# Plain fp32 matmuls in the Fourier transforms of a Hyena branch, in place of three matmuls of split operands

## The chip, the cores and the metric

The kernel runs on one core of one Trainium2 chip. A core has TensorE (PE, matrix products; PEld is its weight load), VectorE (DVE), ScalarE (ACT), GpSimd (POOL) and SyncE (SP, which here issues nearly all DMA transfers). The metric is the device time of one execution in microseconds, as the median of three runs.

## The reference

One layer of an encoder trunk on x of shape (1, 1024, 1024), in fp32. Three token mixers (A: windowed attention, B: Hyena, C: differential attention) read one normed input projection; their outputs are gated, summed and projected, and a SwiGLU feed-forward part follows. The change touches branch B alone:

```python
def hyena_filters(L, w1, b1, f1, w2, b2, f2, w3):
    ...
    h = jnp.sin(f1.astype(f32) * (z @ w1.astype(f32) + b1.astype(f32)))
    h = jnp.sin(f2.astype(f32) * (h @ w2.astype(f32) + b2.astype(f32)))
    h = (h @ w3.astype(f32)).reshape(L, HY_ORDER, HY_DIRS, HY_WIDTH)
    ...
    h = h * decay[:, None, None, :]
    fwd, bwd = h[:, :, 0], h[:, :, 1]
    c = jnp.concatenate([fwd[:1] + bwd[:1], fwd[1:], jnp.zeros_like(fwd[:1]), bwd[1:][::-1]], axis=0)
    return c * lax.rsqrt(jnp.sum(c * c, axis=0, keepdims=True) + RMS_EPS)

def fft_conv(u, cf):
    L = u.shape[1]
    U = jnp.fft.rfft(u.astype(jnp.float32), n=2 * L, axis=1)
    y = jnp.fft.irfft(U * cf[None], n=2 * L, axis=1)[:, :L]
    return y.astype(u.dtype)

def hyena_branch(u, conv_w, conv_b, w1, b1, f1, w2, b2, f2, w3, hy_d):
    L = u.shape[1]
    u = short_conv(u, conv_w, conv_b)
    v, x1, x2 = jnp.split(u, 3, axis=-1)
    cf = jnp.fft.rfft(hyena_filters(L, w1, b1, f1, w2, b2, f2, w3), axis=0)
    z = x1 * (fft_conv(v, cf[:, 0]) + hy_d[0] * v)
    z = x2 * (fft_conv(z, cf[:, 1]) + hy_d[1] * z)
    return z
```

L is 1024, the branch is 512 channels wide, and there are two orders, so two filters and two convolutions of 512 channels.

## The kernel before

**Arithmetic.** Nearly every product is made with fp32r operands, each fp32 operand split into a high and a low part: `split` (lines 98 to 100) lets ScalarE write the rounded high part and VectorE (or GpSimd) subtract it from the source; `mm3` (102 to 105) then makes three matmuls, high by high, high by low, low by high. A matmul of plain F32 tiles is possible too and is used in small places (lines 224, 229, 250, 690).

**The transforms.** A transform of length 2048 is taken apart into a radix-16 stage on VectorE and ScalarE (`fwd`, lines 107 to 159) and dense products with tables of cosines and sines on TensorE (`dft`, 161 to 181). The 512 channels are worked on as two halves of 256. For each half, `fwd` makes four groups of sources: od (two groups, lines 136 and 137), ev (147 to 149) and e0 (151 to 157). `dft` splits a group into rh and rl, loads for each of its two residues a table `ft`, and makes eight products of 128x128 weights by 128x256 into a PSUM tile X, each of them by `mm3`. `filters` (240 to 318) does this for two orders by two halves: it makes the filter in time from the features (line 271 and 272) times a decay table `dec` that is loaded, transforms it, and stores the spectrum H to DRAM (`hd`).

**The convolutions.** `hyena` (495) runs order by order and half by half. `conv` (320 to 398) transforms its input with `fwd`; for each group it loads H, multiplies it with X on VectorE into m1 (328 to 338), splits m1 into yh and yl (340), loads the inverse tables `it` (344) and makes eight products into a PSUM tile V (347 and 348), which VectorE and ScalarE then put together (350 to 398). In all there are 32 forward groups (16 of filters, 16 of convolutions) and 16 inverse ones.

**Tables.** The tables of the forward and inverse transforms come in as inputs `fw` and `iv`, with the high and low parts side by side (384 KB and 512 KB for each of eight residues). At the beginning GpSimd's queue copies `fw` to an F32R tensor in DRAM (1044 to 1046), and in the second filter it copies `iv` (303 to 305); the loads of `ft` and `it` read these copies. SP's queue issues them in order with all other loads and stores.

**What sets the order.** The framework orders instructions per engine when the kernel is built, by priority and by the order of the program; each engine then works its list off in order, waiting on semaphores. Other work of TensorE is put between the transforms by generators: `E.tick(us)` (989 to 995) draws from `E.fill` half-tiles of the Hyena projection (`hyena_proj`, 459 to 485), of the attention projections (`qkv`, 529 to 601) and of the gates (518), until their nominal costs use up the credit. E.rate sets how much is drawn at each tick: 7.0 in the filters, 5.5 in the convolutions. `hyena_proj` makes u with three VectorE operations (463 and after), and for the tiles of v it turns u by eight transposes (`to_slots`, 487). `qkv` collects in `pend` the rope of a half (541) and runs it at the next half's first step.

**Buffers.** Tiles take turns in a number of buffers by tag. In the filters (1057): rh 2, rl 1, ft 2, k4 4, h4 1. In the convolutions (1062): rh 2, rl 1 (yh and yl use them too), ft 2, it 1, k4 4, u8 2. The transforms' PSUM tiles share three buffers (x).

Of the kernel before, what the change touches and what calls it, by code (L numbers as in the profile page):

```python
# [17 lines left out]

def f22(x):
    x=np.asarray(x,np.float32); u=x.view(np.uint32).astype(np.uint64)  # L20
    u=(u+0x7FF+((u>>12)&1))&~np.uint64(0xFFF)
    return u.astype(np.uint32).view(np.float32)
def hilo(m):
    h=f22(m.astype(np.float32)); l=f22((m-h.astype(np.float64)).astype(np.float32))
    return h,l

def dft_tables():
    n1=np.arange(128)[:,None]; k1=np.arange(128)[None,:]
    fw=np.zeros((8,128,6,128),np.float32)
    iv=np.zeros((8,128,4,256),np.float32)  # L30
    for r in range(1,8):
        ph=2*PI*(n1*(16*k1+r)%2048)/2048
        c,s=np.cos(ph),np.sin(ph)
        ch,cl=hilo(c); sh,sl=hilo(s)
        for i,m in enumerate((ch,cl,sh,sl,-sh,-sl)): fw[r,:,i,:]=m
        g=2.0/2048
        yr=np.concatenate([g*c.T,-g*s.T],1); yi=np.concatenate([g*s.T,g*c.T],1)
        for i,m in enumerate(hilo(yr)+hilo(yi)): iv[r,:,i,:]=m
    kk=np.arange(64)[None,:]
    p0=2*PI*(n1*(16*kk)%2048)/2048; p8=2*PI*(n1*(16*kk+8)%2048)/2048  # L40
    alt=1.0-2.0*(np.arange(128)%2)
    c0,s0,c8,s8=np.cos(p0),np.sin(p0),np.cos(p8),np.sin(p8)
    s0n=s0.copy(); s0n[:,0]=alt

    for i,m in enumerate(hilo(np.concatenate([c0,c8],1))+hilo(np.concatenate([s0n,s8],1))): fw[0,:,i,:]=m
    g=2.0/2048
    z=np.zeros((64,128))
    w=np.full((64,1),g); w[0]=g/2
    yr=np.concatenate([np.concatenate([w*c0.T,z],0),np.concatenate([z,g*c8.T],0)],1)
    yi=np.concatenate([np.concatenate([w*s0n.T,z],0),np.concatenate([z,g*s8.T],0)],1)  # L50
    for i,m in enumerate(hilo(yr)+hilo(yi)): iv[0,:,i,:]=m
    return fw,iv

def dft_tables2():
    fw,iv=dft_tables()
    f=np.zeros((8,128,768),np.float32)
    f[1:]=fw[1:].reshape(7,128,768)
    p=np.zeros((128,4,192),np.float32)
    p[:,:,0:64]=fw[0,:,0:4,0:64]; p[:,:,128:192]=fw[0,:,0:4,64:128]
    f[0]=p.reshape(128,768)  # L60
    return f,iv.reshape(8,128,1024)
def filt_tables():
# [18 lines left out]
def dma(nc,dst,src):  # L81
    f=lambda t: t.bitcast(F32) if t.dtype==F32R else t
    nc.sync.dma_start(f(dst),f(src))
# [77 lines left out]
def dft(nc,E,pool,gi,src):  # L161

    hi=pool.tile([128,2,2,256],F32R,tag="rh",name="rh"); lo=pool.tile([128,2,2,256],F32R,tag="rl",name="rl")
    split(nc,hi,lo,src,E.loeng(gi))
    X=E.px.tile([128,2,2,256],F32,tag="x",name="X")
    for i,r in enumerate(GROUPS[gi]):
        t=pool.tile([128,768],F32R,tag="ft",name="ft")
        dma(nc,t,E.fw[r])
        if r==0:
            w=t.rearrange("p (a b) -> p a b",b=192)  # L170
            for k,(a,b) in enumerate(((0,1),(2,3))):
                mm3(nc,X[:,i,k,:],w[:,a,0:128],w[:,b,0:128],hi[:,0,0,:],lo[:,0,0,:],True,False)
                mm3(nc,X[:,i,k,:],w[:,a,64:192],w[:,b,64:192],hi[:,1,0,:],lo[:,1,0,:],False,True)
        else:
            w=t.rearrange("p (a b) -> p a b",b=128)
            R=(hi[:,0,i,:],lo[:,0,i,:]); J=(hi[:,1,i,:],lo[:,1,i,:])
            mm3(nc,X[:,i,0,:],w[:,0],w[:,1],R[0],R[1],True,False)
            mm3(nc,X[:,i,0,:],w[:,4],w[:,5],J[0],J[1],False,True)
            mm3(nc,X[:,i,1,:],w[:,0],w[:,1],J[0],J[1],True,False)
            mm3(nc,X[:,i,1,:],w[:,2],w[:,3],R[0],R[1],False,True)  # L180
    return X
# [58 lines left out]
def filters(tc,nc,E,a,h2):  # L240
    V=nc.vector
    if True:
      with tc.tile_pool(name="fl",bufs=1,reuse_waits="tile",side="right") as fl_:
# [8 lines left out]
        for o in range(2):  # L252
          for u in range(2):
# [42 lines left out]
            def consume(gi,X):  # L296
                H=fl.tile([128,2,2,256],F32,tag="h4",name="H")
                nc.scalar.copy(H,X)
                if gi==3:
                    dma(nc,E.hd[o][u][1:128,4096:4352],H[1:128,0,0,:])  # L300
                    dma(nc,E.hd[o][u][0:1,4096:4352],H[0:1,0,1,:])
                    z=nc.gpsimd.memset(H[0:1,0,1,:],0.0)
                    if o==0 and u==1:
                        with tc.issue_after(z.ins):
                            for r in range(8): nc.gpsimd.dma_start(E.iv[r],a['iv'][r])
                dma(nc,E.hd[o][u][:,1024*gi:1024*gi+1024],H.rearrange("p a b c -> p (a b c)"))
# [13 lines left out]
def conv(nc,E,cv,u8,o,u,ysb):  # L320
# [3 lines left out]
    def consume(gi,X):  # L324
# [13 lines left out]
        V.tensor_tensor(m1[:,:,1,:],m1[:,:,1,:],m2[:,:,0,:],op=ALU.add)  # L338
        yh=cv.tile([128,2,2,256],F32R,tag="rh",name="yh"); yl=cv.tile([128,2,2,256],F32R,tag="rl",name="yl")
        split(nc,yh,yl,m1,E.loeng(gi))  # L340
        P=E.px.tile([128,2,2,256],F32,tag="x",name="V")
        for i,r in enumerate(GROUPS[gi]):
            t=cv.tile([128,4,256],F32R,tag="it",name="it")
            dma(nc,t.rearrange("p a b -> p (a b)"),E.iv[r])
            for c in range(2):
                s=slice(128*c,128*c+128)
                mm3(nc,P[:,i,c,:],yh[:,i,0,s],yl[:,i,0,s],t[:,0],t[:,1],True,False)
                mm3(nc,P[:,i,c,:],yh[:,i,1,s],yl[:,i,1,s],t[:,2],t[:,3],False,True)
        E.tick(E.rate)
# [109 lines left out]
def hyena_proj(tc,nc,E,prep,a,hT):  # L459
# [3 lines left out]
    STT=lambda o,a,s,b: V.scalar_tensor_tensor(o,a,s,b,op0=ALU.mult,op1=ALU.add)  # L463
    st={}
    for t,h in [(4,0),(5,0),(4,1),(5,1)]+[(t,h) for t in (6,7,8,9,0,1,2,3,10,11) for h in range(2)]:
# [13 lines left out]
        if h:  # L479
            if t<4:  # L480
                dma(nc,E.vc[0][t//2][:,t%2,:],u)
                to_slots(nc,E,E.gp,E.px.tile([128,8,128],F32,tag="x",name="pv"),u,lambda s: dma(nc,E.vd[t//2][:,:,128*(t%2):128*(t%2)+128],s))
            else:
                dma(nc,E.x12[(t-4)//2][:,t%2,:],u)
        yield 5.45

# [42 lines left out]
def qkv(tc,nc,E,prep,a,hT,pool):  # L529
# [37 lines left out]
    def group(c0,nh,T,qk,vd):  # L567
# [3 lines left out]
        for h in range(2):  # L571
            X=E.gp.tile([128,4,4,64],F32,tag="gt",name="X")
            if vd: vh=pool.tile([128,4,128*n],F32R,tag="th",name="vh"); vl=pool.tile([128,4,128*n],F32R,tag="tl",name="vl")
            for tp in range(2):
                p=E.pg.tile([128,2,256],F32,tag="g",name="pN")
                for t in range(2):
                    for q in range(4):
                        s=slice(256*tp+128*t,256*tp+128*t+128)
                        for k in range(2):
                            mm3(nc,p[:,t],hT[h][0][:,2*q+k,s],hT[h][1][:,2*q+k,s],W[q][0][:,k],W[q][1][:,k],q+k==0,q+k==4)  # L580
                ts=slice(2*tp,2*tp+2)
                with tc.high_priority(HP):
                    nc.scalar.copy(X[:,ts].rearrange("p t s d -> p t (s d)"),p)
                if vd: split(nc,vh[:,ts],vl[:,ts],X[:,ts,nh:4].rearrange("p t s d -> p t (s d)"),nc.gpsimd)
                if tp==0:
                    while pend: pend.pop()()
                yield 5.76
            if vd:
                for i in range(n):
                    for d,v in zip(vd[i],(vh,vl)): dma(nc,d[:,4*h:4*h+4],v[:,:,128*i:128*i+128])  # L590
            if nh: pend.append(lambda h=h,X=X: rope(h,X[:,:,0:nh],T,qk))
    pend=[]
    for gn,jobs in (('qn_c',[(3+i,4,[E.cqk[2*i+j][0] for j in range(2)],None) for i in range(2)]),
# [5 lines left out]
        for c0,nh,qk,vd in jobs:  # L599
            yield from group(c0,nh,T,qk,vd)  # L600
    pend.pop()()

# [381 lines left out]
def encoder(tc,a,out):  # L984
    nc=tc.nc
    E=E_()
    E.loeng=lambda gi: nc.vector
    E.fill=[]; E.credit=0.0; E.rate=0.0
# [14 lines left out]
    with ExitStack() as top:  # L1003
# [3 lines left out]
        E.hd=[[D(f"hd{o}{u}",[128,4352]) for u in range(2)] for o in range(2)]  # L1007
        E.fw=[D(f"fw{r}",[128,768],F32R) for r in range(8)]; E.iv=[D(f"iv{r}",[128,1024],F32R) for r in range(8)]
        E.vd=[D(f"vd{u}",[128,8,256]) for u in range(2)]
# [23 lines left out]
        with ExitStack() as z:  # L1033
            feat=[]; mlp=filter_mlp(tc,nc,E,a,fst,feat)
            m0=pool(z,"m0",{'xt':8,'xn':2,'ssr':3,'ssq':2})
            late=m0.tile([128,1],F32,tag="late",name="late")
            xs=[]
            with tc.high_priority(3*HP):
                for i in range(8):
                    t=m0.tile([128,1024],F32,tag="xt",name="xt"); dma(nc,t,x[128*i:128*i+128]); xs.append(t)  # L1040
                    if i==0:
                        dma(nc,E.ident,a['ident'])
                        g=m0.tile([128,1024],F32,tag="g",name="g"); dma(nc,g,a['norm1_g'].broadcast_to([128,1024]))
            seen=nc.gpsimd.tensor_copy(late,xs[7][:,0:1])
            with tc.issue_after(seen.ins):
                for r in range(8): nc.gpsimd.dma_start(E.fw[r],a['fw'][r])
            next(mlp)
# [5 lines left out]
        with ExitStack() as hy:  # L1053
            qp=pool(hy,"qp",{'m2':1,'ssq':2,'ssr':3,'th':1,'tl':1})
            D0=hyena_proj(tc,nc,E,prep,a,hT); D2=qkv(tc,nc,E,prep,a,hT,qp); D1=gates(tc,nc,E,prep,a,hT)
            E.fill=[D0,D2,D1]
            E.flb={'k4':4,'u8':2,'wr':1,'wa':2,'wb':2,'k2':4,'k2a':2,'h4':1,'rs':3,'rh':2,'rl':1,'ft':2,'fg':1,'od':1}
            E.rate=7.0
            filters(tc,nc,E,a,feat)
            fst.close()  # L1060
            drain(D0)
            cv=pool(hy,"cv",{'u8':2,'k2':11,'k4':4,'h4':1,'rh':2,'rl':1,'ft':2,'it':1,'fg':1,'od':1},side="right")
            E.rate=5.5
# [73 lines left out]
def tables():  # L1137
    t={}
    t['fw'],t['iv']=dft_tables2()
    t['zT'],t['decay']=filt_tables()  # L1140
# [21 lines left out]
```

## Time and profile before

| what | value |
|---|---|
| median of 3 runs | 2219.35 us (2217.25 to 2220.83) |
| the profiled execution | 2214.34 us |
| its span, first to last instruction | 2212.6 us |
| busy: PE, PEld, DVE, ACT, POOL | 1980.1, 1658.8, 1414.3, 876.0, 444.6 us |
| mean granted TensorE clock | 0.960 |

The times below are those of the profiled execution. In a row of the profile the line number is that of the kernel before; where a helper makes the instruction (L99 and L100 for `split`, L103 to L105 for `mm3`, L83 for the DMAs), the tiles tell which call it is: `X<-rh,ft` is a product of a forward transform, `V<-it,yh` one of an inverse one. A row "A <- B: 27.1, 11, 10.6" says that A stood idle for 27.1 us in 11 times, until B was done, 10.6 us the longest time. In a row of the order in time the columns are start, duration, engine, line, instruction, tiles (out<-in), shape, and in brackets the idle time just before it with what ended it. In the view of busy time by stretch, each engine has its busy time and in brackets its number of instructions; the last columns are the granted clock, the share of the time in which the DMA engines were busy, and the rate.

### The profile page before, as it was taken

What the parts mean: (1) busy time and instruction counts of PE and PEld (TensorE: products, weight loads), DVE (VectorE), ACT (ScalarE), POOL (GpSimd) and SP (SyncE); (2) the same over time, 40 slices, a digit from 0 to 9 for tenths busy, and PEclk for the clock granted to TensorE, in tenths of its full rate; (3) what the DMA queues carried; (4) which work ended last, traced back from release to release, by engine and by line L of the source; (5) the groups of instructions that cost most, each with busy time, mean ns of one, the idle gap of its engine ahead of it and who ended that gap; (6) DMA issues with size and microseconds to landing.
All of it is one profiled execution on the core that took longest, in us unless ns stands there. A gap on an engine that the chain in (4) does not pass through costs nothing. (4 is left out here: it accounts for less than half of the span.)

```text
span 2212.6 us, 27550 instructions
## 1 busy us (share of the span) xinstructions
PE 1980.1 (89%) x10597; PEld 1658.8 (75%) x10597; DVE 1414.3 (64%) x2019; ACT 876.0 (40%) x1371; POOL 444.6 (20%) x302
## 2 busy tenths in 40 slices
PE   6986888888868999899879988899699999999999
PEld 4775788888867778677668766699488888888887
DVE  7875777775775654642467877534856656557674
ACT  5433333333332222765666654234422222223332
POOL 2532232212141112432000023400210110101000
PEclk9999999999989999999889999899799999999999
DMA  5457536575556556334354342444222322248333
GB/s 194 143 189 244 191 94 221 163 228 183 179 202 204 188 177 189 95 103 92 94 157 118 119 135 72 147 166 159 67 95 96 110 105 100 95 157 313 116 109 104
DMA packets 141454, 327.28 MB, mean 148 GB/s; under 512 B 18518, under 2 KB 44616, under 8 KB 139530
## 3 DMA queue, kind: packets, MB, share of 16 engines
q1 hardware_dynamic: 140810, 318.17, 44.6%
q0 software_dynamic: 512, 7.34, 0.9%
q8 instruction: 83, 1.36, 0.3%
q14 instruction: 49, 0.40, 0.1%
HBM read 237.65 MB, written 95.16 MB: 150 GB/s over the span
## 5 line engine op out<-in xcount | busy, mean ns | idle before, releaser
L427 POOL TENSOR_TENSOR wlo<-wraw,whi 128x512 fp32r<-128x512 f32 x96 | 142.0, 1482 | 625.4 <-ACT whi L426 590.4
L103 PE MATMUL pT<-hT,whi 128*128 128x512 f32 x576 | 233.8, 406 | 19.1 <-DVE u L463 10.6
L105 PE MATMUL pT<-hT,wlo 128*128 128x512 f32 x576 | 232.3, 403 | 0.0
L104 PE MATMUL pT<-hT,whi 128*128 128x512 f32 x576 | 231.7, 402 | 0.6 <-DVE hT L100 0.6
L426 ACT ACTIVATE whi<-wraw 128x512 fp32r<-128x512 f32 (+1 forms) x148 | 99.5, 675 | 217.5 <-PE pT L104 110.0
L103 PE MATMUL pN<-whi,hT 128*128 128x256 f32 x576 | 164.5, 286 | 12.3 <-ACT whi L426 12.0
L104 PE MATMUL pN<-wlo,hT 128*128 128x256 f32 x576 | 164.5, 286 | 5.6 <-DVE wlo L427 5.5
L105 PE MATMUL pN<-whi,hT 128*128 128x256 f32 x576 | 163.5, 285 | 0.0
L103 PE MATMUL fp<-S,bh 128*128 128x512 f32 x352 | 141.5, 402 | 7.7 <-ACT bh L99 7.7
L103 PEld LDWEIGHTS pT<-hT,whi 128*128 128x128 f32 x576 | 112.1, 195 | 45.1 <-issue 18.1
L105 PE MATMUL fp<-S,bh 128*128 128x512 f32 x352 | 139.0, 395 | 0.0
L104 PE MATMUL fp<-S,bh 128*128 128x512 f32 x352 | 139.0, 395 | 0.0
L104 PEld LDWEIGHTS pT<-hT,whi 128*128 128x128 f32 x576 | 112.0, 194 | 24.8 <-issue 1.5
L105 PEld LDWEIGHTS pT<-hT,wlo 128*128 128x128 f32 x576 | 111.7, 194 | 23.1
L103 PEld LDWEIGHTS pN<-whi,hT 128*128 128x128 f32 x576 | 112.5, 196 | 13.7 <-ACT whi L426 13.2
L105 PE MATMUL fo<-w2h,gA 128*128 128x512 f32 x308 | 119.8, 389 | 0.0
L104 PE MATMUL fo<-w2h,gA 128*128 128x512 f32 x308 | 119.8, 389 | 0.0
L103 PE MATMUL fo<-w2h,gA 128*128 128x512 f32 x308 | 119.7, 389 | 0.0
L104 PEld LDWEIGHTS pN<-wlo,hT 128*128 128x128 f32 x576 | 112.7, 196 | 6.7 <-DVE wlo L427 6.6
L105 PEld LDWEIGHTS pN<-whi,hT 128*128 128x128 f32 x576 | 112.7, 196 | 0.0
L103 PE MATMUL X<-rh,ft 128*128 128x256 f32 x256 | 79.1, 309 | 37.5 <-ACT rh L99 27.1
L99 ACT ACTIVATE bh<-t 128x1024 fp32r<-128x1024 f32 x44 | 46.5, 1059 | 145.3 <-PE fp L104 142.8
(347 smaller groups left out, 5395.4 us busy)
## 6 DMA issues: line engine op xcount, KB each, us to landing
wraw<-in_w SPq DMA_DIRECT2D x108, 256.0 KB, 3.2
ft<-fw SPq DMA_DIRECT2D x64, 384.0 KB, 4.2
graw<-gs SPq DMA_DIRECT2D x35, 512.0 KB, 3.5
it<-iv SPq DMA_DIRECT2D x32, 512.0 KB, 3.7
gd<-gt SPq DMA_DIRECT2D x24, 512.0 KB, 3.0
gt<-gd SPq DMA_DIRECT2D x24, 512.0 KB, 3.2
wraw<-in_ffn_w SPq DMA_DIRECT2D x22, 512.0 KB, 3.7
r<-in_ffn_w SPq DMA_DIRECT2D x22, 512.0 KB, 3.6
```

Of the source, the lines that this page charges most:

```text
L99: nc.scalar.activation(hi,src,AF.Identity)
L103: nc.tensor.matmul(p,lh,rh,start=first,stop=False)
L104: nc.tensor.matmul(p,lh,rl,start=False,stop=False)
L105: nc.tensor.matmul(p,ll,rh,start=False,stop=last)
L426: nc.scalar.activation(hi,raw,AF.Identity)
L427: (eng or nc.vector).tensor_tensor(lo,raw,hi.bitcast(F32),op=ALU.subtract)
```

## The change

The forward products, the inverse products and their tables become plain fp32. The tables hold each value once (192 KB and 256 KB for a residue in place of 384 KB and 512 KB) and are read from the inputs; the two copies on GpSimd's queue, with the small copy that the first one waited for, are gone. `dft` takes the source group itself as the moving operand, and `conv` takes m1 as the stationary one: rh, rl, yh and yl, with 48 splits, no longer exist. Each `mm3` there becomes one matmul call.

Buffers change with it. Filters: k4 6, h4 2, ft 3, no rh and rl. Convolutions: u8 3, k4 5, it 2, no rh and rl.

Two steps are issued later than before: in `hyena_proj` the transposes of a finished tile of v come after the first half-tile of the next tile, and in `qkv` the rope of a half comes at the second step of the next half instead of its first, and one rope at a time, oldest first.

The features and the weights of the filters (lines 232 to 236, 259 to 263) are split as before, as are all other products.

```diff
@@ def dft_tables():
-    fw=np.zeros((8,128,6,128),np.float32)
-    iv=np.zeros((8,128,4,256),np.float32)
+    fw=np.zeros((8,128,384)); iv=np.zeros((8,128,2,256))
...
-        ch,cl=hilo(c); sh,sl=hilo(s)
-        for i,m in enumerate((ch,cl,sh,sl,-sh,-sl)): fw[r,:,i,:]=m
...
+        fw[r]=np.concatenate([c,s,-s],1)
@@ def dft(nc,E,pool,gi,src):
-    hi=pool.tile([128,2,2,256],F32R,tag="rh",name="rh"); lo=pool.tile([128,2,2,256],F32R,tag="rl",name="rl")
-    split(nc,hi,lo,src,E.loeng(gi))
     X=E.px.tile([128,2,2,256],F32,tag="x",name="X")
+    mm=nc.tensor.matmul
     for i,r in enumerate(GROUPS[gi]):
-        t=pool.tile([128,768],F32R,tag="ft",name="ft")
+        t=pool.tile([128,384],F32,tag="ft",name="ft")
         dma(nc,t,E.fw[r])
...
-            R=(hi[:,0,i,:],lo[:,0,i,:]); J=(hi[:,1,i,:],lo[:,1,i,:])
-            mm3(nc,X[:,i,0,:],w[:,0],w[:,1],R[0],R[1],True,False)
-            mm3(nc,X[:,i,0,:],w[:,4],w[:,5],J[0],J[1],False,True)
-            mm3(nc,X[:,i,1,:],w[:,0],w[:,1],J[0],J[1],True,False)
-            mm3(nc,X[:,i,1,:],w[:,2],w[:,3],R[0],R[1],False,True)
+            R,J=src[:,0,i,:],src[:,1,i,:]
+            mm(X[:,i,0,:],t[:,0:128],R,start=True,stop=False)
+            mm(X[:,i,0,:],t[:,256:384],J,start=False,stop=True)
+            mm(X[:,i,1,:],t[:,0:128],J,start=True,stop=False)
+            mm(X[:,i,1,:],t[:,128:256],R,start=False,stop=True)
@@ def filters(tc,nc,E,a,h2):
-                    z=nc.gpsimd.memset(H[0:1,0,1,:],0.0)
-                    if o==0 and u==1:
-                        with tc.issue_after(z.ins):
-                            for r in range(8): nc.gpsimd.dma_start(E.iv[r],a['iv'][r])
+                    nc.gpsimd.memset(H[0:1,0,1,:],0.0)
@@ def conv(nc,E,cv,u8,o,u,ysb):
-        yh=cv.tile([128,2,2,256],F32R,tag="rh",name="yh"); yl=cv.tile([128,2,2,256],F32R,tag="rl",name="yl")
-        split(nc,yh,yl,m1,E.loeng(gi))
...
-            t=cv.tile([128,4,256],F32R,tag="it",name="it")
+            t=cv.tile([128,2,256],F32,tag="it",name="it")
...
-                mm3(nc,P[:,i,c,:],yh[:,i,0,s],yl[:,i,0,s],t[:,0],t[:,1],True,False)
-                mm3(nc,P[:,i,c,:],yh[:,i,1,s],yl[:,i,1,s],t[:,2],t[:,3],False,True)
+                nc.tensor.matmul(P[:,i,c,:],m1[:,i,0,s],t[:,0],start=True,stop=False)
+                nc.tensor.matmul(P[:,i,c,:],m1[:,i,1,s],t[:,1],start=False,stop=True)
@@ def hyena_proj(tc,nc,E,prep,a,hT):
-                to_slots(nc,E,E.gp,E.px.tile([128,8,128],F32,tag="x",name="pv"),u,lambda s: dma(nc,E.vd[t//2][:,:,128*(t%2):128*(t%2)+128],s))
+                pend.append(lambda t=t,u=u: to_slots(nc,E,E.gp,E.px.tile([128,8,128],F32,tag="x",name="pv"),u,lambda s: dma(nc,E.vd[t//2][:,:,128*(t%2):128*(t%2)+128],s)))
...
+        elif pend: pend.pop()()
@@ def qkv(tc,nc,E,prep,a,hT,pool):
-                if tp==0:
-                    while pend: pend.pop()()
+                if tp==1 and pend: pend.pop()()
...
-            if nh: pend.append(lambda h=h,X=X: rope(h,X[:,:,0:nh],T,qk))
+            if nh: pend.insert(0,lambda h=h,X=X: rope(h,X[:,:,0:nh],T,qk))
@@ def encoder(tc,a,out):
-        E.fw=[D(f"fw{r}",[128,768],F32R) for r in range(8)]; E.iv=[D(f"iv{r}",[128,1024],F32R) for r in range(8)]
+        E.fw=[a['fw'][r] for r in range(8)]; E.iv=[a['iv'][r] for r in range(8)]
...
-            seen=nc.gpsimd.tensor_copy(late,xs[7][:,0:1])
-            with tc.issue_after(seen.ins):
-                for r in range(8): nc.gpsimd.dma_start(E.fw[r],a['fw'][r])
...
-            E.flb={'k4':4,'u8':2,'wr':1,'wa':2,'wb':2,'k2':4,'k2a':2,'h4':1,'rs':3,'rh':2,'rl':1,'ft':2,'fg':1,'od':1}
+            E.flb={'k4':6,'u8':2,'wr':1,'wa':2,'wb':2,'k2':4,'k2a':2,'h4':2,'rs':3,'ft':3,'fg':1,'od':1}
...
-            cv=pool(hy,"cv",{'u8':2,'k2':11,'k4':4,'h4':1,'rh':2,'rl':1,'ft':2,'it':1,'fg':1,'od':1},side="right")
+            cv=pool(hy,"cv",{'u8':3,'k2':11,'k4':5,'h4':1,'ft':2,'it':2,'fg':1,'od':1},side="right")
```

More of the change, by code (lines that the diff above doesn't have):

```diff
@@ L17 @@
 SLOT=[0,1,2,3,4,7,6,5]
[L19 to L25, printed above, removed]
 def dft_tables():
     n1=np.arange(128)[:,None]; k1=np.arange(128)[None,:]
-    fw=np.zeros((8,128,6,128),np.float32)
-    iv=np.zeros((8,128,4,256),np.float32)
+    fw=np.zeros((8,128,384)); iv=np.zeros((8,128,2,256))
+    g=2.0/2048
     for r in range(1,8):
@@ L33, in dft_tables @@
         c,s=np.cos(ph),np.sin(ph)
-        ch,cl=hilo(c); sh,sl=hilo(s)
-        for i,m in enumerate((ch,cl,sh,sl,-sh,-sl)): fw[r,:,i,:]=m
-        g=2.0/2048
-        yr=np.concatenate([g*c.T,-g*s.T],1); yi=np.concatenate([g*s.T,g*c.T],1)
-        for i,m in enumerate(hilo(yr)+hilo(yi)): iv[r,:,i,:]=m
+        fw[r]=np.concatenate([c,s,-s],1)
+        iv[r,:,0]=np.concatenate([g*c.T,-g*s.T],1); iv[r,:,1]=np.concatenate([g*s.T,g*c.T],1)
     kk=np.arange(64)[None,:]
     p0=2*PI*(n1*(16*kk)%2048)/2048; p8=2*PI*(n1*(16*kk+8)%2048)/2048
-    alt=1.0-2.0*(np.arange(128)%2)
     c0,s0,c8,s8=np.cos(p0),np.sin(p0),np.cos(p8),np.sin(p8)
[L43 to L61, printed above, removed]
+    s0[:,0]=1.0-2.0*(np.arange(128)%2)
+    o=np.zeros((128,64))
+    fw[0]=np.concatenate([c0,o,c8,s0,o,s8],1)
+    z=np.zeros((64,128)); w=np.full((64,1),g); w[0]=g/2
+    iv[0,:,0]=np.concatenate([np.concatenate([w*c0.T,z],0),np.concatenate([z,g*c8.T],0)],1)
+    iv[0,:,1]=np.concatenate([np.concatenate([w*s0.T,z],0),np.concatenate([z,g*s8.T],0)],1)
+    return fw.astype(np.float32),iv.reshape(8,128,512).astype(np.float32)
 def filt_tables():
@@ L161, in dft @@
 def dft(nc,E,pool,gi,src):
-    hi=pool.tile([128,2,2,256],F32R,tag="rh",name="rh"); lo=pool.tile([128,2,2,256],F32R,tag="rl",name="rl")
-    split(nc,hi,lo,src,E.loeng(gi))
     X=E.px.tile([128,2,2,256],F32,tag="x",name="X")
+    mm=nc.tensor.matmul
     for i,r in enumerate(GROUPS[gi]):
-        t=pool.tile([128,768],F32R,tag="ft",name="ft")
+        t=pool.tile([128,384],F32,tag="ft",name="ft")
         dma(nc,t,E.fw[r])
         if r==0:
[L170 to L173, printed above, removed]
-        else:
-            w=t.rearrange("p (a b) -> p a b",b=128)
-            R=(hi[:,0,i,:],lo[:,0,i,:]); J=(hi[:,1,i,:],lo[:,1,i,:])
-            mm3(nc,X[:,i,0,:],w[:,0],w[:,1],R[0],R[1],True,False)
-            mm3(nc,X[:,i,0,:],w[:,4],w[:,5],J[0],J[1],False,True)
-            mm3(nc,X[:,i,1,:],w[:,0],w[:,1],J[0],J[1],True,False)
-            mm3(nc,X[:,i,1,:],w[:,2],w[:,3],R[0],R[1],False,True)
+            for k in range(2):
+                mm(X[:,i,k,:],t[:,192*k:192*k+128],src[:,0,0,:],start=True,stop=False)
+                mm(X[:,i,k,:],t[:,192*k+64:192*k+192],src[:,1,0,:],start=False,stop=True)
+        else:
+            R,J=src[:,0,i,:],src[:,1,i,:]
[3 more added lines that the diff above has]
+            mm(X[:,i,1,:],t[:,128:256],R,start=False,stop=True)
     return X
@@ L463, in hyena_proj @@
     STT=lambda o,a,s,b: V.scalar_tensor_tensor(o,a,s,b,op0=ALU.mult,op1=ALU.add)
-    st={}
+    st={}; pend=[]
     for t,h in [(4,0),(5,0),(4,1),(5,1)]+[(t,h) for t in (6,7,8,9,0,1,2,3,10,11) for h in range(2)]:
@@ L600, in qkv @@
             yield from group(c0,nh,T,qk,vd)
-    pend.pop()()
+    while pend: pend.pop()()
 def load_stack(nc,dst,src,swap=False):
@@ L986, in encoder @@
     E=E_()
-    E.loeng=lambda gi: nc.vector
     E.fill=[]; E.credit=0.0; E.rate=0.0
@@ L1035, in encoder @@
             m0=pool(z,"m0",{'xt':8,'xn':2,'ssr':3,'ssq':2})
-            late=m0.tile([128,1],F32,tag="late",name="late")
             xs=[]
@@ L1138, in tables @@
     t={}
-    t['fw'],t['iv']=dft_tables2()
+    t['fw'],t['iv']=dft_tables()
     t['zT'],t['decay']=filt_tables()
```

## The prediction

> **What bounds the kernel now.** I read three views: where the transforms lie in time and the busy time of each engine by stretch; then TensorE's own waits between 100 and 860 us; then the order in time at a few places.
>
> ```profile
> L103 PE MATMUL X<-rh,ft x256: 274/283/584, 111.0 to 815.1; 128*128 128x256 f32 x128
> L105 PE MATMUL V<-it,yl x128: 277/282/415, 405.2 to 835.5; 128*128 128x256 f32 x128
> ```
> ```profile
> core 0: us, PE busy (x) PEld busy (x) DVE busy (x) ACT busy (x) POOL busy (x), PEclk, DMA share, GB/s
> 100.00:360.00 260.00, 212.38 (x1316) 188.07 (x1317) 181.47 (x240) 94.92 (x142) 79.33 (x58) 0.93 0.55 181
> 360.00:700.00 340.00, 278.72 (x2065) 262.94 (x2065) 243.82 (x372) 106.11 (x170) 85.65 (x55) 0.93 0.60 196
> 700.00:850.00 150.00, 141.58 (x716) 118.41 (x715) 88.75 (x143) 41.81 (x68) 27.68 (x18) 0.97 0.56 184
> ```
>
> The products into X (forward transforms) and V (inverse ones) lie between 111 and 836 us: filters up to about 360, convolutions after that. In the three stretches TensorE (PE) is busy 632.7 of 750 us and idle 117.3; VectorE (DVE) is busy 514.0. Neither is full: TensorE takes its work in a fixed order and stands still when the next operand is late. What comes after 850 us holds nothing of the change and starts when the convolutions are done, so I move it as a block. What the idle time is made of (us in total, times, the longest):
>
> ```profile
> PE X L103 <- ACT rh L99: 27.1, 11, 10.6
> PE pN L103 <- ACT whi L426: 12.0, 5, 5.2
> PE V L103 <- DMA it<-iv: 11.1, 12, 2.5
> PE pv L489 <- DVE u L463: 10.9, 1, 10.9
> PE pT L103 <- DVE u L463: 10.6, 3, 6.4
> PE pt L561 <- POOL X L556: 10.2, 6, 3.7
> PE X L103 <- DMA ft<-fw: 9.0, 10, 2.4
> ...
> PE X L104 <- DVE rl L100: 5.1, 4, 2.2
> ...
> PE V L105 <- DVE yl L100: 2.3, 3, 1.3
> PE V L103 <- ACT yh L99: 1.9, 3, 1.2
> ```
>
> The splits (rh, rl, yl, yh) hold 36.4 us of it, the table loads (it, ft) 20.1.
>
> **TensorE: two passes for three, but dearer ones.** Records overlap (0.28 us long and 0.12 apart below), so I count from start to start.
>
> ```profile
> 136.84 0.28 PE L271 MATMUL pc<-wa,hs 128*128 128x256 f32 x1
> ...
> 137.79 0.40 PE L105 MATMUL pT<-hT,wlo 128*128 128x512 f32 x1
> 138.02 0.39 PE L103 MATMUL pT<-hT,whi 128*128 128x512 f32 x1
> ...
> 138.72 0.50 PE L250 MATMUL pn<-ones,q 128*128 128x1 f32 x4
> 139.09 0.48 PE L103 MATMUL pT<-hT,whi 128*128 128x512 f32 x1
> ```
> ```profile
> 1130.72 1.02 PE L690 MATMUL prs<-odg,one 128*128 128x512 f32 x2
> 1131.58 0.60 PE L659 MATMUL T<-ident,e 128*128 128x128 f32 x4
> ```
>
> From 136.84 to 137.79 eight fp32r passes of 256 columns start (seven are left out): 0.119 us each. A pass of 512 takes 0.23. The plain fp32 matmul L690 is one call in the code and two records, with 0.86 us for both: 0.43 per pass of 512. The trace has no plain pass of 256 columns. It can't be less than that of one column: the two plain matmuls of L250 are four such passes in 0.37 us, about 0.09 each. It can't be more than the 0.43 of 512. I take half of that, 0.215, since the fp32r pass halves too (0.23 to 0.119). One product then costs 2 x 0.215 = 0.43 where three passes cost 0.357. There are 256 products into X and 128 into V (the counts above), so 384 x 0.073 = 28 us more; at the granted clock of 0.93 about **+30 us**. The ends: 2 x 0.09 makes each product 0.18 cheaper (-68 us), 2 x 0.43 makes it 0.50 dearer (+193). The value taken lies by the nearest row, the 512-column one of the same kind, and I give the ends little chance.
>
> **The splits.** Each transform group loses an activation and a subtraction:
>
> ```profile
> L99 ACT ACTIVATE rh<-od x16: 1041/1052/1062, 109.9 to 761.4; 128x1024 fp32r<-128x1024 f32 x16
> L100 DVE TENSOR_TENSOR rl<-od,rh x16: 1209/1224/2843, 111.1 to 768.6; 128x1024 fp32r<-128x1024 f32 x16
> L99 ACT ACTIVATE rh<-ev x8: 1043/1058/1062, 118.6 to 791.4; 128x1024 fp32r<-128x1024 f32 x8
> L100 DVE TENSOR_TENSOR rl<-ev,rh x8: 1209/1215/1228, 122.0 to 793.5; 128x1024 fp32r<-128x1024 f32 x8
> L99 ACT ACTIVATE rh<-e x8: 1042/1056/1064, 123.0 to 810.2; 128x1024 fp32r<-128x1024 f32 x8
> L100 DVE TENSOR_TENSOR rl<-e,rh x8: 1215/1226/1716, 127.9 to 811.3; 128x1024 fp32r<-128x1024 f32 x8
> ```
> ```profile
> L99 ACT ACTIVATE yh<-m x16: 1040/1060/1067, 402.8 to 820.6; 128x1024 fp32r<-128x1024 f32 x16
> L100 DVE TENSOR_TENSOR yl<-m,yh x16: 1212/1225/1227, 403.9 to 823.9; 128x1024 fp32r<-128x1024 f32 x16
> ```
>
> (Durations: least/median/most, in ns.) VectorE loses 48 subtractions of 1.22 us, 59 us; ScalarE 48 activations of 1.05, 50 us. In what TensorE waits for, the hop goes but not what stands ahead of it. The longest wait shows this:
>
> ```profile
> 653.87 1.74 DVE L137 TENSOR_TENSOR od<-A,B 128x1024 f32<-128x1024 f32 x1
> 656.73 1.74 DVE L100 TENSOR_TENSOR rl<-od,rh 128x1024 fp32r<-128x1024 f32 x1 [1.12 <-ACT rh L99]
> ```
>
> od ends at 655.6 and the product starts only 1.1 us later, after 10.6 us of idle time; od itself was late, and od will be the name of the wait afterwards. The ten other waits of rh mean (27.1 - 10.6)/10 = 1.65 us, not far above the hop's own length. So I take from the 36.4 us: 9.3 for rl, yl and yh less 1; 1.1 of the longest; and 12 of the other 16.5, hence **-21 us** (ends: 0 if od and m are as late as rh and yh were, and -36). VectorE's 59 us come free on an engine that is 69% busy here (514.0 of 750). Of the waits on things that pass through VectorE or ScalarE beside the transforms (whi, and u before pT: 12.0 + 10.6 = 22.6) I take a third: **-8** (ends 0 and -23).
>
> **Tables from the inputs.** Two copies on GpSimd's queue go: fw early, iv beside the second filter. The second shows what it costs:
>
> ```profile
> 200.00:219.00 19.00, 8.06 (x36) 6.47 (x35) 4.84 (x5) 5.28 (x9) 4.54 (x9) 0.80 0.93 320
> ```
> ```profile
> DVE c L275 <- DMA dec<-in_decay: 15.1, 2, 9.3
> ```
> ```profile
> iv<-in_iv POOLq DMA_DIRECT2D x8, 512.0 KB, 8.4
> ```
>
> In these 19 us the DMA engines are 93% busy, the filters' decay tables come late, VectorE stands for 15.1 us in the same window, and TensorE behind it is busy 8.06 us; the 10.9 us wait for u (pv L489) is its end. The copy reads 4.2 MB and writes as much. Without it, and with the transposes pv set one half-tile later by the change, I expect **-13 us**: the 10.9, and some of the half-speed clock (0.80) after it. Ends: -4, if hd, decay and weights crowd the queues anyway, and -15. The early copy I cost at nothing: no row among the waits names it.
>
> **Buffers and moved steps.** `it` gets a second buffer and its load is half as long, `ft` is halved and has three buffers in the filters: of their 20.1 us I take **-16** (ends -8, -20). SP's queue, which issues all loads in order, is also held less by them. The rope of a half is issued one step later and one at a time: of the 10.2 us for `X L556` **-4** (ends +4, since transposes that come later may meet other work, and -10). A buffer now held longer is od, m, ev or e0 (until the products have run, in place of until the split): the convolutions have five k4 buffers for four, the filters six for four, and the pool of one od is refilled only at the next transform, so I cost this at nothing; if that cover is missing, VectorE waits some 0.6 us per group (a group's eight products, 3.4 us for 2.9), 48 x 0.6 = 29 us on an engine with slack.
>
> **The clock and new waits.** The granted clock of 0.93 in 100 to 700 means 14% of the time at half speed. If idle time falls by half, some 0.02 of it comes back on 491 us of busy TensorE: **-8** (ends 0, -20). Against that, where a stall goes the next operand is late: od, m, H, weights (whi). I give back **+8** (ends 0, +25).
>
> Sum: 30 - 21 - 8 - 13 - 16 - 4 - 8 + 8 = **-32 us**. The profiled execution takes 2214.34 us, its span 2212.6; the median shown is 2219.35, 5 us above. I add the sum to the median: **2187 us** (profiled: 2182).
>
> **The rivals.**
> 1. *The waits only change name* (od for rh, m for yh): VectorE's chain sets the pace, as the 10.6 us wait shows in one place. Then +30 stands against the copy (-13), the tables (-16) and a little of the rest (-8): 2212. For it: VectorE is 69% busy in chains. Against it: that chain loses rl and yl, 59 us.
> 2. *TensorE nearly full*: all named waits of splits and tables go, the clock stays up, and weights come early: 30 - 36 - 20 - 13 - 15 - 15 = -69, so 2150. It has for it that 117 us are idle; against it, that many waits have a second cause close behind.
> 3. *Slower, as TensorE is the bound where the stage is packed.* In 700 to 850 it is idle 8.4 of 150 us, and there nothing hides dearer passes. If filters and convolutions run as packed after the change because the scheduler's order puts the same fillers between them, the 30 us count whole and only the tables' waits go partly (-10): 2239. It decides from the point at which less than 30 of the 117 us are won back.
> 4. *Weight loads that no longer hide.* Each plain pass loads its own weights, 768 against 1152 times. If 0.09 us (L250) came on top of every pass: 768 x 0.09 = 69 us on the forecast, 2256. L690 speaks against it: its second load is inside the 0.86 us. The Trainium skill ("TensorE: Matmul & The Clock Gate", section "Weight-path perf modes") says that the fast weight load is off for FP32 inputs, which speaks for slower loads here; by its figure for a load, 128 columns at 1.2 per ns, one would take 0.107 us (an estimate). The trace agrees in size (0.09 in L250), and that still lies under a pass of 0.215.
>
> **How the numbers follow.** Forecast (-32, from -50 to -12): 0.60. Rival 1: 0.17. Rival 2: 0.12. Rival 3: 0.08. Rival 4: 0.03. The range reaches from between rival 2 and the forecast, 2160, to just past rival 1, 2215; outside are most of rival 2 and rivals 3 and 4. A measurement of this kernel can tell some 0.2% (4.4 us) from no change. Of rival 1, 0.06 falls within that; slower are rivals 3 and 4 and a bit of 1, 0.12; faster is the rest, 0.82.
>
> **What would show it.** Records into X and V: 768 in place of 1152, 0.21 us apart (0.12 or 0.43 would be the bounds). No rh, rl, yh, yl; TensorE's waits for od and m should be under 16 us together; over 30 is rival 1. No stretch near 200 us with TensorE under half busy; waits for it and ft under 5 us. VectorE's busy time in the three stretches lower by about 59 us, ScalarE's by 50. The last V some 32 us before 835.5, and what follows shifted as a block; if the part after 850 changes its length by more than 6 us, my frame is wrong.

## The result, and the profile after

The changed kernel takes 2160.8 us (median of 4 runs, 2157.19 to 2163.98), the kernel before 2220.09 beside it: a ratio of 0.9734, 95% interval 0.9713 to 0.9755. The forecast was 2187 us with a range of 2160 to 2215. The time lies 0.8 us inside the fast end of the range, less than the width of the interval, and the gain of 59 us is nearly twice the 32 forecast. Rival 2 of the prediction had 2150 us, nearer to the measured time than the forecast is. The profiled execution has a span of 2158.6 us.

The page's busy times (us, share of the span, instructions):

```profile
PE 1986.1 (92%) x10213; PEld 1657.4 (77%) x10213; DVE 1341.5 (62%) x1971; ACT 839.4 (39%) x1331; POOL 438.7 (20%) x285
```

The same three stretches as before; the last V now starts at 767.9 us:

```profile
100.00:360.00 260.00, 222.98 (x1215) 193.31 (x1214) 168.45 (x234) 81.08 (x129) 84.04 (x54) 0.93 0.44 146
360.00:700.00 340.00, 310.94 (x2023) 285.91 (x2023) 242.65 (x405) 93.34 (x163) 90.01 (x56) 0.96 0.57 187
700.00:850.00 150.00, 145.98 (x658) 119.13 (x657) 60.38 (x131) 47.83 (x89) 35.74 (x23) 1.00 0.51 149
```
```profile
L317 PE MATMUL V<-it,m x128: 378/379/483, 387.6 to 767.9; 128*128 128x256 f32 x128
```

TensorE is idle 70.1 us in them where it was idle 117.3 (the times are the same, the work in them is not: the changed kernel is further along). From 200 to 220 us, where the hole was, it is busy the whole time. Its waits between 100 and 790 us:

```profile
PE pt L531 <- POOL X L526: 19.5, 4, 9.6
PE pT L80 <- DVE u L432: 13.5, 3, 5.6
PE pN L81 <- DVE wlo L396: 6.5, 3, 3.3
PE X L151 <- issue: 6.5, 5, 2.8
PE pN L80 <- ACT ss L225: 5.4, 1, 5.4
PE X L151 <- DVE od L113: 2.8, 2, 2.2
...
PE V L317 <- DVE m L309: 1.6, 1, 1.6
PE X L151 <- DMA ft<-in_fw: 1.1, 1, 1.1
PE V L316 <- DVE m L308: 1.0, 1, 1.0
```

Where rh, rl, yl and yh held 36.4 us, od and m hold about 5, or about 12 if the 6.5 us of X are theirs too, for which the profile names nothing that was waited for ("issue"); the wait for `it` is gone, that for `ft` nearly. What grew most is the wait of the rope's transposes (pt, 10.2 to 19.5). The products into X and V are 768 records where they were 1152. A plain pass, in the order in time of TensorE (start, duration, and two passes to a row):

```profile
388.10 0.59 PE L316 MATMUL V<-it,m 128*128 128x256 f32 x2
388.53 0.59 PE L317 MATMUL V<-it,m 128*128 128x256 f32 x2
388.96 0.59 PE L316 MATMUL V<-it,m 128*128 128x256 f32 x2
```

Each product takes 0.43 us, as half of the 512-column pass had said.

**The end of the transforms moves further than the end of the kernel.** The last V starts 835.5 - 767.9 = 67.6 us earlier, the span ends 54.0 us earlier. The matmuls pT (Hyena's and the gates' projections, the fillers) up to the last V and behind it, before and then after the change:

```profile
0.00:835.50 835.50, 270.66 (x1080) 207.38 (x1081) 36.90 (x60) 31.29 (x57) 0.94 0.57 187
835.50:2212.60 1377.10, 167.89 (x648) 121.84 (x648) 0.00 (x0) 15.79 (x27) 0.97 0.39 124
```
```profile
0.00:767.90 767.90, 237.19 (x960) 185.24 (x961) 37.17 (x60) 28.46 (x52) 0.95 0.49 163
767.90:2158.60 1390.70, 199.85 (x768) 142.71 (x768) 0.00 (x0) 18.92 (x32) 0.97 0.40 125
```

120 of them (120 x 0.23 = 27.6 us) have slid past the last V. They are all that slid: the count of all matmul records behind it grows by 119 (6243 to 6362). The rest of the program is 1390.7 - 1377.1 = 13.6 us longer. So of the 67.6 us, 27.6 is filler that had not been done yet, and the rest of the program takes half of that into its own gaps.

### The profile page after: what moved, and what is told of

Read it like the earlier page. It is cut to its first block, busy times and chain, and to the rows that moved or that the text cites. A ratio compares the mean times of both kernels' runs of the same rounds, so it can differ in the third digit from the quotient of the medians.

```text
span 2158.6 us, 26632 instructions
## 1 busy us (share of the span) xinstructions
PE 1986.1 (92%) x10213; PEld 1657.4 (77%) x10213; DVE 1341.5 (62%) x1971; ACT 839.4 (39%) x1331; POOL 438.7 (20%) x285
## 4 chain that ended last, share of the span: by engine, by line
PE 50%; DVE 5%; ACT 2%; POOL 2%; DMA 2%; issue 1%; SPq 0%; POOLq 0%; ACTq 0%; DVEq 0%
PE fp L82 5%; PE fp L81 5%; PE fp L80 5%; PE fo L82 3%; PE fo L81 3%; PE fo L80 3%; PE S L614 2%; PE f L82 2%; PE f L81 2%; PE f L80 2%; PE pw L81 1%; PE pw L82 1%; PE pw L80 1%; PE pT L81 1%; PE pT L80 1%; PE pT L82 1%
## 5 line engine op out<-in xcount | busy, mean ns | idle before, releaser
L615 DVE TENSOR_REDUCE mx<-S 128x1 f32<-128x1024 f32 x64 | 77.9, 1220 | 46.6 <-PE S L614 45.8
```

What stands on the lines that cost most here:

```text
L615: V.reduce_max(mx[:,c:c+1],S,axis=AX.X)
```

## The experiments

All times are medians, the ratios are against the kernel before on the same chip, with 95% intervals. The changed kernel itself stands at 0.9734.

**The two moved steps.** First both undone, in the changed kernel:

```diff
-                pend.append(lambda t=t,u=u: to_slots(...))
+                to_slots(...)
-        elif pend: pend.pop()()
...
-                if tp==1 and pend: pend.pop()()
+                if tp==0:
+                    while pend: pend.pop()()
...
-            if nh: pend.insert(0,lambda h=h,X=X: rope(h,X[:,:,0:nh],T,qk))
+            if nh: pend.append(lambda h=h,X=X: rope(h,X[:,:,0:nh],T,qk))
```

> The changed kernel (2160.8 us) with its two moved steps put back: the transposes pv right after the tile u, the rope at the next half's first step, all that wait at once. Theory A (the moves are worth little, the gain is in splits, copy and buffers): 2155 to 2168. The wait of pt for POOL X, 19.5 us in the changed kernel and 10.2 before, goes back to about 10, and the wait of pv for u grows from 2.4 us to about 8. Rival (the moved steps made part of the gain that the forecast missed, 27 us): 2172 or more.

Measured: 2196.77 us, 0.9889 (0.986 to 0.9918). The moves were worth some 36 us of the 59, in this kernel: the rival, and more than it asked for. The wait of pt did not go back to 10 us but rose to 45.9; that of pv for u is 7.2, as expected. Then only the rope put back:

```diff
-                if tp==1 and pend: pend.pop()()
+                if tp==0:
+                    while pend: pend.pop()()
...
-            if nh: pend.insert(0,lambda h=h,X=X: rope(h,X[:,:,0:nh],T,qk))
+            if nh: pend.append(lambda h=h,X=X: rope(h,X[:,:,0:nh],T,qk))
```

> The changed kernel with only the rope put back to the next half's first step; the transposes pv stay late. Theory B (the 45.9 us of waits of pt for POOL X with both moves undone are the price): 2185 to 2198, with that wait at 40 us or more. Rival (the transposes pv, which stand in TensorE's order in the filters, are the price): 2158 to 2170.

Measured: 2189.27 us, 0.9868 (0.9849 to 0.9887). So 28 us belong to the rope alone, and the transposes pv have what is left of the 36, about 7, which the intervals don't separate from nothing. The waits of TensorE in this run:

```profile
PE pt L531 <- POOL X L526: 44.7, 10, 7.8
PE pT L80 <- DVE u L432: 12.7, 3, 5.2
```

44.7 us for pt where the kernel before had 10.2 and the changed one 19.5: the difference of 25 us to the changed kernel is nearly the whole price of 28. The same steps moved in the kernel before:

> The kernel before with only the two moved steps of the change (transposes pv one half-tile later, one rope at a time at the second step). Theory B (the moves are worth what their undoing cost, 36 us, on their own): 2180 to 2190. Rival (the moves pay only where the splits are gone, since in the kernel before other waits, rh and it, stand in the same places): 2208 to 2222.

Measured: 2204.64 us, 0.994 (0.9922 to 0.9959), which is 13 us by the ratio (16 by the medians) and between the two theories. The waits there:

```profile
PE X L103 <- ACT rh L99: 19.5, 8, 4.9
...
PE V L103 <- DMA it<-iv: 13.7, 12, 4.0
...
PE pt L562 <- POOL X L557: 3.3, 3, 2.5
```

In the kernel before, the rope's result is waited for 10.2 us; with the rest of the change in and the rope where it was, for 44.7. So the move is worth more in the changed kernel (36 us, both steps) than in the kernel before (13 us). A likely reading is that TensorE in the kernel before stands for the splits and the tables in the same stretches, and that the rope catches up meanwhile. No run tests this alone: that would take the old place of the rope with the splits' hop still there.

**The buffers.** All numbers of before, in the changed kernel:

```diff
-{'k4':6,'u8':2,...,'h4':2,'rs':3,'ft':3,'fg':1,'od':1}
+{'k4':4,'u8':2,...,'h4':1,'rs':3,'ft':2,'fg':1,'od':1}
-{'u8':3,'k2':11,'k4':5,'h4':1,'ft':2,'it':2,'fg':1,'od':1}
+{'u8':2,'k2':11,'k4':4,'h4':1,'ft':2,'it':1,'fg':1,'od':1}
```

> The changed kernel with the numbers of buffers of before (filters: k4 4, h4 1, ft 2; convolutions: u8 2, k4 4, it 1). Theory A: the halved loads alone don't hide the single buffer of it, so V waits for it again for 6 to 10 us, and the total is 2168 to 2175 (8 to 14 us of the gain is the buffers'). Rival (buffers held until the products have run make VectorE wait, or SP's queue stands behind them): 2185 or more. Other rival (half the bytes are enough): 2158 to 2164.

Measured: 2184.42 us, 0.9839 (0.981 to 0.9868): 24 us, more than the first theory gave and just short of the rival. TensorE's waits (100 to 840 us):

```profile
PE X L151 <- issue: 17.1, 5, 7.1
PE pN L81 <- DVE wlo L396: 9.6, 4, 7.8
PE V L316 <- DMA it<-in_iv: 9.2, 8, 2.5
PE X L151 <- DVE od L113: 9.2, 3, 5.2
```

The single it is late again for 9.2 us even at half the bytes, as the first theory had it. The first products of the transforms wait longer too ("issue" 17.1 us for 6.5, od 9.2 for 2.8). Three runs part the buffers. First it and ft kept as changed, the rest as before:

> The changed kernel with the buffers of the kernel that kept the hop (filters: k4 4, h4 1, ft 3; convolutions: u8 2, k4 4, it 2), products straight from the sources. Beside the 2183.4 us with the hop it gives the hop alone (ScalarE's 50 us, VectorE's 59 us, and two steps in the chain). Theory D (the hop itself is worth little, the buffers that fit in its memory are the gain): 2176 to 2185. Rival A (the hop is worth the 21 + 8 us of the prediction): 2150 to 2160.

Measured: 2165.1 us, 0.9749 (0.9729 to 0.977). It lies between the two theories, nearer to rival A. So it and ft carry 2184.4 - 2165.1 = 19 us together (no run parts the two), and k4, h4 and u8 together about 4, which is within the measurement. The two others agree:

> The changed kernel with two buffers of u8 in the convolutions in place of three. Undoing all buffers cost 24 us. Theory D1 (the third u8 lets the next half's v be loaded and its radix stage run while y of the last half is still in use; without it X waits some 5 us at each of four halves): 2175 to 2182. Rival (k4 or it carry the 24 us): 2158 to 2167.

Measured: 2162.8 us, 0.9734 (0.9713 to 0.9755): the third u8 does nothing that can be seen.

> The changed kernel with four buffers of k4 in the convolutions in place of five; m1, ev and e0 are now held until the products have run. Theory D1: 2158 to 2166 (TensorE runs the products soon after, so the slot is free in time). Rival (the fifth k4 carries most of the 24 us): 2173 to 2184.

Measured: 2164.12 us, 0.9744 (0.9726 to 0.9762): neither does the fifth k4. m1, ev and e0 being held longer costs nothing.

**The hop.** Plain products as in the change, but from copies:

```diff
+def hop(nc,pool,src):
+    h=pool.tile([128,2,2,256],F32,tag="rh",name="rh"); l=pool.tile([128,2,2,256],F32,tag="rl",name="rl")
+    nc.scalar.activation(h,src,AF.Identity)
+    nc.vector.tensor_tensor(l,src,h,op=ALU.max)
+    return h,l
```

> The changed kernel, but each source of a product first goes through a copy on ScalarE (rh, yh) and one on VectorE (rl, yl) of the same size as the splits were, and half of the products wait for each; products plain as in the changed kernel. Buffers of before, but it 2 and ft 3 in the filters. Theory A (the hop in the chain and VectorE's 59 us are the largest part of the gain): 2190 to 2205, with X waiting for rh 20 us and more. Rival (the waits only change name, since VectorE's chain is as late without the hop): 2165 to 2175, all of it from the buffers.

Measured: 2183.4 us, 0.9838 (0.981 to 0.9866); neither theory. Its own buffers without the hop are the 2165.1 us above (0.9749). The hop alone is worth 18 us, against theory D, which had put it near nothing. TensorE's waits in it:

```profile
PE X L158 <- ACT rh L140: 12.5, 7, 3.6
...
PE X L159 <- DVE rl L141: 3.7, 3, 2.1
...
PE V L325 <- DVE rl L141: 2.7, 4, 0.9
PE X L154 <- ACT rh L140: 2.1, 2, 1.1
```

These four rows are 21.0 us; the splits' waits were 36.4 before.

**The copies.** The tables copied again on GpSimd's queue, at the new half size (`E.fw` and `E.iv` as DRAM tiles, the `dma_start` loops of before):

> The changed kernel with the two copies of the tables on GpSimd's queue put back, with the new tables of half the size (1.5 and 2.1 MB), loads from the copies. Theory A: the copy beside the second filter delays the decay tables, half as much as before: 6 to 9 us, 2167 to 2170. Rival (the copy only happened beside a stall that hd, decay and weights make alone): 2158 to 2164.

Measured: 2164.92 us, 0.9753 (0.9731 to 0.9776), between the two theories and 0.9 us from the rival's: 4 us, within the measurement. The hole near 200 us does not stand at the same time in every kernel, so I compare TensorE from 180 to 280 us. In this order: the kernel before; the kernel before with only the moved steps, where the copy of iv keeps its full size; the changed kernel with the copies at half size; the changed kernel.

```profile
180.00:280.00 100.00, 78.89 (x442) 67.25 (x440) 55.99 (x76) 35.21 (x53) 20.48 (x20) 0.91 0.69 229
180.00:280.00 100.00, 79.82 (x438) 67.54 (x438) 60.31 (x84) 34.94 (x51) 19.03 (x21) 0.90 0.71 236
180.00:280.00 100.00, 91.92 (x438) 77.26 (x437) 55.97 (x74) 32.06 (x51) 28.21 (x24) 0.95 0.60 192
180.00:280.00 100.00, 94.60 (x490) 80.41 (x489) 59.71 (x81) 33.65 (x53) 24.40 (x17) 1.00 0.56 184
```

TensorE is idle 21.1, 20.2, 8.1 and 5.4 us. The moved steps alone only shift the hole to a later time. In that kernel the decay tables keep VectorE waiting 5.0 us in place of 15.4 (176 to 245 us), and TensorE stands as long all the same, now 14.5 us for u: the late decay tables alone don't make the hole. The copy at half size adds 2.7 us to the idle time here. No run has the copies at full size in the changed kernel or takes them alone out of the kernel before, so what the full-size copies cost stays open.

**The passes.** Sources, m1 and tables as fp32r, without low parts. The first of the two kernels adds the rounded product three times, so its result is not the layer's; it stands for the time alone. Both take the tables from copies.

```diff
+def passes(nc,p,l,r,start,stop):
+    for i in range(3): nc.tensor.matmul(p,l,r,start=start and i==0,stop=stop and i==2)
```

> The changed kernel with each product made by three fp32r matmuls of the same rounded operands (three times the rounded product; sources and m1 are written as fp32r, no low parts), and with the tables copied in DRAM as fp32r, since they are read as that. It takes the dearer passes back without the splits. If TensorE's time counts whole (28 us for 384 products) and the copies cost what e3 showed (4): 2130 to 2143. If VectorE's chain sets the pace and the passes lie beside other waits: 2155 to 2168.

Measured: 2125.2 us, 0.9576 (0.9556 to 0.9597). The plain passes cost 36 us against three of fp32r, or about 40 if the copies' 4 are believed; the time lies 5 us below the lower end of the first forecast (2130). TensorE's busy time, from the two pages, is 1986.1 - 1955.7 = 30.4 us less. So they count whole. Whether they cost more than the 28 to 30 us of TensorE's time isn't clear, with intervals of about 5 us on each side.

> As the kernel with three passes, but with one fp32r matmul for each product (the rounded product). It takes 384 x (0.43 - 0.119) = 119 us of TensorE's time away from the changed kernel. If TensorE's time counts whole: 2040 to 2055. If the chain through VectorE and GpSimd takes over: 2090 to 2140.

Measured: 2076.99 us, 0.9369 (0.9344 to 0.9394). Two passes fewer for each product, 384 x 2 x 0.119 = 91 us of TensorE, save 48: between both theories. The waits of od and wlo (3.0 and 4.0 us in the kernel with three passes) and of ft grow:

```profile
PE pN L81 <- DVE wlo L403: 10.2, 5, 6.1
PE X L139 <- DVE od L113: 9.9, 4, 3.5
...
PE X L139 <- DMA ft<-fw: 7.9, 3, 3.4
```

About half of the TensorE time that was taken away shows as time. This version is the fastest of all, with the transforms' operands rounded to fp32r in place of the reference's full fp32.

**The fillers.** E.rate 6.5 for 5.5 in the convolutions:

> The changed kernel with E.rate 6.5 for 5.5 in the convolutions, which puts more of the gates' half-tiles back between the transforms: at the last V the changed kernel had done 960 of the gates' and Hyena's matmuls pT, the kernel before 1080, and 120 x 0.23 = 27.6 us of work went past it. If that shift is work moved and not saved (13.6 us of it came back as a longer rest): the last V comes 20 to 28 us later, the total stays within 2156 to 2168. Rival (the shift itself is a gain, since attention has room for it): 2170 to 2178.

Measured: 2165.32 us, 0.9758 (0.9733 to 0.9782), not clear of the changed kernel and inside the first theory's range.

The matmuls pT up to its last V and behind it:

```profile
0.00:808.80 808.80, 283.08 (x1152) 221.51 (x1152) 37.23 (x60) 33.18 (x60) 0.95 0.49 160
808.80:2172.60 1363.80, 146.76 (x576) 106.34 (x576) 0.00 (x0) 14.13 (x24) 0.96 0.40 124
```

1152 - 960 = 192 matmuls, 44 us, came back in front of the last V, which is 40.9 us later (20 to 28 were expected, for 120 matmuls); the rest is 26.9 us shorter. The profiled execution is some 9 us above this kernel's median, so between 4 us (medians) and 14 us (spans) of the shift is saved; most of it is work moved, but a small gain isn't excluded.

## Why the prediction was right, and where its sum was not

The direction held, and so did the mechanisms of the passes, the splits and the table buffers. The range held by 0.8 us only, and that is luck: the sum was too small by 27 us, because one term (the rope) was far too small, while others (the copy, the splits, perhaps the passes) were off the other way. Rival 2 was nearer in the number, and in the waits too: those of splits and tables fell from 56.5 us to about 7, or 13 with the "issue" rows. But it did not name the rope either.

- **Two dearer passes.** The length of a pass was right (0.43 us for a product). The term of +30 fits TensorE's busy time (30.4 us); the time says 36 to 40, which is not clear of 30. The weight loads hide, as the 0.43 shows, so rival 4 is out. Rival 3 was right in one thing, that TensorE's time counts whole, and wrong in that less than this would be won back.
- **Splits and the relief of VectorE, -21 and -8.** The hop, which puts back both the chain and the load of ScalarE and VectorE, measured 18 us where the two terms had 29. The waits of TensorE for whi and for u before pT, of which the second term took 8 us, are 20.1 us with the hop and 15.2 without it (100 to 840 us, same buffers).
- **The copy, -13.** The hole went, but no run shows that the copy's going took it. The prediction read the hole at 200 us as the copy's, because the copy ran in it and the decay tables were late. The copies cost 4 us at half size, within the measurement. With the full copy and decay tables only 5.0 us late, TensorE was idle as long as before. The size of this term is not borne out, and how much of the hole the full-size copy made stays open.
- **it and ft, -16.** About right: the buffers alone are 19 us, with the wait for it gone in the changed kernel. The term also meant the halved loads. No run has plain products with tables of full size, so their part isn't measured.
- **Other buffers, nothing.** Right: about 4 us in sum, within the measurement.
- **The rope, -4.** This term was the largest error: 28 us. Its bounds (+4 and -10) came from the 10.2 us that TensorE waited for it in the kernel before. That row says what the rope cost in the kernel before, not what it would cost in the changed one. The prediction gave back +8 for "new waits" and named od, m, H and whi, but not the rope, which is where the new wait would have stood (44.7 us) and which the change had moved partly out of the way. That is rival 1's mechanism, at another place.
- **The clock, -8.** The granted clock in the three stretches went from 0.93, 0.93 and 0.97 to 0.93, 0.96 and 1.00. TensorE's busy time in the whole program rose by 6.0 us only (1980.1 to 1986.1), though the products alone cost some 28 more. The higher clock fits this; no run measures its part.
- **od and m under 16 us, it and ft under 5:** both held (5 to 12 us and about 1).
- **The block after 850 us.** Wrong, by the prediction's own test: it grew by 13.6 us. The order made when the kernel is built put 120 filler matmuls fewer before the last V. It is not the splits' going that does it: with the hop kept there are 960 before the last V too, as with the moved steps undone, the copies back, three passes or one. Only undoing all buffers (979) and raising E.rate (1152) change the number. Which part of the change sets it stays open.
- **The forecast of busy times.** VectorE loses 1414.3 - 1341.5 = 72.8 us in the whole program for 59 forecast, ScalarE 876.0 - 839.4 = 36.6 for 50. The 14 us more of VectorE are not explained. The stretches can't be compared, since the changed kernel is further along in the last of them.

Undone one by one in the changed kernel, the parts are worth 36 (moves), 24 (buffers) and 4 (copies), and 18 (hop, beside the smaller buffers); less 40 for the passes that is 42 us of the 59. They are not independent: the moves alone gave 13 us in the kernel before and cost 36 to undo. Where the other 17 us come from stays open: from pairs of these, or from the halved tables, which every run of the changed kernel keeps.

## What to carry to other kernels

The price of a wait in a profile is its price beside the other waits of the same stretch; before removing some, ask which short wait in the same engine's order would be the long one then, and move that too. What a stage gains must be read with the work that was done in it: count the fillers before and after the mark, or a shift of work looks like a saving. A transfer that runs inside a hole has not thereby made the hole. A kernel with the transfer put back at its full size would tell; look for the hole over a long stretch, since it may only have moved.

## What was not expected of the hardware

ScalarE saved 14 us less than its 48 activations (36.6 of 50 us). Its instructions fell by 40, not 48: the loads of its function tables rose from 38 to 46, and each takes 1.28 us. They grew where the gates and the two attentions run side by side, and they go with the gates' matmuls that stand behind the last V. With 648 pT matmuls there (the kernel before) the loads are 38, with 768 (the changed kernel) 46, and with 576 (E.rate 6.5, the only edit in that run) 32. The rows of the three places where this shows, before and then after (the gates' activation, and the exponentials of the two attentions):

```profile
L525 ACT ACT_TABLE_LOAD x15 | 19.2, 1283 | 4.0 <-DMA gd<-gt 3.7
L740 ACT ACT_TABLE_LOAD x7 | 9.0, 1283 | 5.7 <-DVE amx L738 5.6
L649 ACT ACT_TABLE_LOAD x6 | 7.7, 1283 | 2.8 <-DVE mx L647 2.7
```
```profile
L495 ACT ACT_TABLE_LOAD x19 | 24.4, 1283 | 1.8 <-DMA gd<-gt 1.5
L709 ACT ACT_TABLE_LOAD x9 | 11.5, 1283 | 3.7 <-DVE amx L707 3.6
L618 ACT ACT_TABLE_LOAD x9 | 11.5, 1283 | 6.3 <-DVE mx L616 6.2
```

Here they are 28 before and 37 after, in the other places 10 and 9: in sum 8 more, or 8 x 1.28 = 10.3 us. The other 3.5 us are not explained.
